# Opening stage of a hybrid decoder layer: load order, the engine that scales x, and instructions kept in program order

## The chip, the cores and the metric

The kernel runs on one core of one Trainium2 chip. The metric is the device time of one execution in microseconds; runs are compared by their medians. The core has five engines with an instruction queue each: PE (TensorE, matmuls), DVE (VectorE), ACT (ScalarE), POOL (GpSimd) and SP (SyncE, which here only issues DMAs). POOL issues DMAs too.

## The reference, cut to what matters

One decoder layer on x of shape 256 tokens x 2048 channels, all in float32. The part that the change touches computes the first normalised and modulated input u:

```python
mod = silu(c) @ w_mod + b_mod              # c: one row of 2048; w_mod: 2048 x 12288
shift1, scale1, ... = split(mod, 6)
u = rms(x, norm1_w) * (1.0 + scale1) + shift1
proj = u @ w_in                            # 2048 x 18464: q, k, v of both mixers, gates, b and a
qkv_b = silu(causal_depthwise_conv(proj[qkv], conv_w))
beta = sigmoid(proj[b]);  g = -exp(a_log) * softplus(proj[a] + dt_bias)
```

After it come two token mixers (stick-breaking attention and a gated delta rule), their merge through `p_a`, `p_b` and `w_out`, and a SwiGLU feed-forward part. Every element of the output depends on u.

## The kernel before, in words

All large products are done as three matmuls on pairs of reduced-precision parts. An operand `a` is split into `ah` (a cast, on ACT) and `al = a - ah` (a subtraction, on DVE). A weight block of 256 x 512 is loaded as `raw`, cast to `wh` (`split_hi`, line 304) and subtracted to `wl` (`split_lo`, through the helper at line 121). One such block is a **step**: 24 matmuls of 256 columns. `raw`, `wh` and `wl` have four buffers each, so the split of step n needs the matmuls of step n-4 to be finished. Buffers of one tag are handed out in program order: the cast of step n+1 is never issued ahead of the cast of step n.

`scale1` and `shift1` are wanted per channel, down the partitions, so they are not made by a wide matmul. Function `u_sums` loads w_mod block by block (`smod`, 512 KB each, issued by POOL at line 407, nine buffers) and adds it up on DVE with the entries of silu(c) as scalars: 16 sums for each of four quarters of the channels (`PIECES`). The even blocks go to `acc01`, the odd ones to `accb`. After the sixteenth sum of a quarter, 32 small matmuls with a column of ones (`pb_mod`) bring the sums to the partitions, and three small DVE operations finish `mcols`. `u_piece(p)` then applies them to the transposed x (`xT`) on ACT, casts to `uh` on ACT and subtracts to `ul` on DVE. I call the quarters 0 to 3, and the sums of quarter p "sum 0 to 15 of quarter p".

x itself is loaded (`xs`, 2 MB), squared and summed on ACT, the reciprocal root is taken on POOL (line 173), x is scaled (line 471, DVE), transposed by 32 matmuls (`pb_u`) and copied to `xT` by ACT (line 480). Small loads of the same stage are `wba` (the 32 columns of w_in for b and a: 2048 pieces of 128 bytes), `crow` (conv_w, transposed on PE to `cw`, copied by DVE at line 460) and `adt` (a_log, dt_bias).

The projections that need u while it is made are the **outer** steps of `run_jobs`, 36 in number. Steps 0 to 11 take channels 0 to 1023 for q, k and v of head group 1; at the ends of steps 9 to 11 their partial results are parked. Steps 12 to 35 take all channels for q, k and v of head group 0. `u_piece(0)` is written at step 0, `u_piece(1)` at step 6, `u_piece(2)` at step 24 and `u_piece(3)` at step 27 (`HK`); the first use of quarter 3 is at step 30. Between the matmuls of the outer steps the program writes the sums of the next quarter: three per step or a little fewer, one or two after each half step. For quarter 3, sums 0 to 2 are written in step 24, 3 to 5 in step 25, 6 and 7 in step 26, and 8 to 15 are written out in full by `u_piece(3)` in step 27. In each step n, the split of step n+1 is written first.

Step 33 finishes q of head group 0. Its `done` calls `open_phase` (masks, and `gdn_scalars`: small ACT, DVE and PE operations for beta and g, ending in the tables exp/ln) and then writes the whole convolution of that q: four ACT scalings, twelve DVE multiply-adds, two Silu on ACT (`gq`). The split of step 35 is written right after it, at the top of step 34.

The order in which each engine executes is set by a planner when the program is built: it issues an instruction on its engine as soon as its inputs are ready in the planner's own forecast of the run, and among several ready ones the first in the program. So an instruction may stand ahead of others that were written earlier. `tc.keep_in_program_order(ins)` puts `ins` behind the instruction that was written just before it on the same engine; nothing is said of the instructions around. An engine's queue, once planned, is executed strictly in that order. `xs` uses the same pool of six large buffers as `acc01` and `accb`, which are asked for earlier, so in the kernel before its load stands behind the first sums in the plan.

Of the kernel before, what the change touches and what calls it, by code (L numbers as in the profile page):

```python
# [38 lines left out]
H2 = 5  # L39
RG = 2  # L40
SMA = 8
NS0 = 4
NS1 = 4
PIECES = ((0, 4), (4, 4), (8, 4), (12, 4))
HK = (0, 0, 0, 2)
HOP = 3
# [51 lines left out]
def body(tc, cst, x, c, w_mod, b_mod, norm1_w, w_in, q_norm_w, k_norm_w, conv_w, a_log, dt_bias,  # L98
# [25 lines left out]
        nc.vector.scalar_tensor_tensor(out=o, in0=a, scalar=s, in1=b, op0=op0, op1=op1, **kw)  # L124

    def act(o, i, f, **kw):
        nc.scalar.activation(out=o, in_=i, func=f, **kw)

    def f32(t):
        return t.bitcast(F32)  # L130
# [158 lines left out]
    def run_jobs(jobs, bg_every=0, outer=(), bg_from=0):  # L289
        steps = [(j, q) for group in outer for q in range(group[0].kt // 2) for j in group]  # L290
        n_outer = len(steps)
        steps += [(j, q) for j in jobs for q in range(j.kt // 2)]
        ns = len(steps)
        raws, splits = {}, {}

        def load(n, queue=nc.sync):
            j, q = steps[n]
            r = wp.tile([P, 2, 512], F32, tag="raw", name="raw", bufs=RAWS)
            queue.dma_start(out=r, in_=j.w[j.kb * P + q * 256:j.kb * P + (q + 1) * 256, j.c0:j.c0 + 512].rearrange("(k p) n -> p k n", p=P))
            raws[n] = r  # L300

        def split_hi(n):
            wh = wp.tile([P, 2, 512], F32R, tag="wh", name="wh", bufs=WB)
            nc.scalar.copy(out=wh, in_=raws[n])  # L304
            splits[n] = (wh,)

        def split_lo(n):
            wl = wp.tile([P, 2, 512], F32R, tag="wl", name="wl", bufs=WB)
            wh = splits[n][0]
            tt(wl, raws.pop(n), f32(wh), ALU.subtract)  # L310
            if n + RAWS < ns:
                load(n + RAWS)
            splits[n] = (wh, wl)

        for n in range(min(RAWS, ns)):
            load(n, nc.gpsimd if outer and n >= RG else nc.sync)
        split_hi(0)
        split_lo(0)
        tick = 0
        for n, (j, q) in enumerate(steps):  # L320
            if n == n_outer:
                for i in range(1, SA):
                    split_hi(n + i)
                    split_lo(n + i)
            if q == 0:
                if j.before:
                    j.before()
                while len(convs) > 1:
                    pump_conv()
                j.acc = [bank("acc", j.tag) for _ in range(4 if j.wide else 2)]  # L330
            wh, wl = splits.pop(n)
            acc = j.acc
            own = n >= n_outer

            def beat(t):

                if own:
                    if t == SPA and n + SA < ns:
                        split_hi(n + SA)
                    if t == SPB and n + SA < ns:  # L340
                        split_lo(n + SA)
                    pump_conv()
                    pump(j.pump)

            if not own and n + 1 < ns and n + 1 not in splits:
                split_hi(n + 1)
                split_lo(n + 1)
            for kk in range(2):
                k = q * 2 + kk
                if k in j.hooks:  # L350
                    j.hooks[k]()
                ah, al = j.act()
                ka = j.kb + k
                first, last = k == 0, k == j.kt - 1
                for b in range(2):
                    beat(2 * kk + b)
                    if j.wide:

                        for cb in (2 * b, 2 * b + 1):
                            s = slice(cb * P, (cb + 1) * P)  # L360
                            mm(acc[cb], wh[:, kk, s], ah(ka), first, False)
                            mm(acc[cb][:, 0:T], wl[:, kk, s], al(ka), False, last)
                    elif j.chan:
                        for cb in (2 * b, 2 * b + 1):
                            o = acc[b][:, (cb % 2) * T:(cb % 2 + 1) * T]
                            s = slice(cb * P, (cb + 1) * P)
                            mm(o, wh[:, kk, s], ah[:, ka], first and cb % 2 == 0, False)
                            mm(o, wh[:, kk, s], al[:, ka], False, False)
                            mm(o, wl[:, kk, s], ah[:, ka], False, last)
                    else:  # L370
                        s = slice(b * P, (b + 1) * P)
                        mm(acc[b], ah[:, ka, s], wh[:, kk], first, False)
                        mm(acc[b], al[:, ka, s], wh[:, kk], False, False)
                        mm(acc[b], ah[:, ka, s], wl[:, kk], False, last)
                if n < n_outer and sums:
                    next(sums[0], None)
                    if tick % 3 == 0:
                        next(sums[0], None)
                if not own:
                    pump(j.pump)  # L380
                tick += 1
                if bg_every and j.bg and tick >= bg_from and tick % (bg_every if j.kt != KT or not j.wide else 2) == 0:
                    pump_bg()
            if q == j.kt // 2 - 1:
                j.done(acc)
# [27 lines left out]
    def u_sums(pi):  # L413
# [3 lines left out]
        for g in range(KT // kg):  # L417
            load_smod(SMA)
            t = smod[pi, g]
            smod[pi, g] = None  # L420
            for kk in range(kg):
                k = kg * g + kk
                a = (acc01, accb)[k % 2][:, :, c0:c0 + cn]
                if k < 2:
                    nc.vector.tensor_scalar(out=a, in0=t[:, :, kk], scalar1=cc[:, k:k + 1], scalar2=None, op0=ALU.mult)
                else:
                    stt(a, t[:, :, kk], cc[:, k:k + 1], a, ALU.mult, ALU.add)
            yield
        for i0 in range(0, kn, 2):
            pm = bank("pb_mod")  # L430
# [9 lines left out]
            tt(mcols[:, 1, kr], pm[:, 0:128:64], bsh1[:, kr], ALU.add)  # L440
        yield

    sums = [u_sums(0)]
    for _ in range(NS0):
        next(sums[0])
    xs = big.tile([P, NB, D], F32, tag="s16", name="xs")
    nc.sync.dma_start(out=xs, in_=xv)
    wba = tps.tile([P, KT, 32], F32, name="wba")
    nc.sync.dma_start(out=wba, in_=w_in[:, OFF_BA:OFF_BA + 32].rearrange("(k p) n -> p k n", p=P))
    for i in range(2):  # L450
        nc.sync.dma_start(out=crow[:, i], in_=conv_w.rearrange("a (k p) -> (a k) p", p=P)[i * 96:(i + 1) * 96])
    adt = cp.tile([P, 2, H], F32, name="adt")
    nc.sync.dma_start(out=adt[:, 0], in_=a_log.partition_broadcast(P))
    nc.sync.dma_start(out=adt[:, 1], in_=dt_bias.partition_broadcast(P))

    cw = cp.tile([P, 2, 96], F32, name="cw")
    pc = bank("pb_cw")
    for i in range(2):
        nc.tensor.transpose(pc[:, i * 96:(i + 1) * 96], crow[:, i], ident[:96, :96])
    nc.vector.tensor_copy(out=cw, in_=pc[:, 0:192])  # L460
    cwv = cw.rearrange("p a b -> p (a b)")

    ss = cp.tile([P, 4, 8], F32, name="ss")
    xT = s16("xT")
    rstd1 = cp.tile([P, 2], F32, name="rstd1")
    for b in range(NB):
        act(xT[:, b * 8:(b + 1) * 8].rearrange("p k t -> p (k t)"), xs[:, b], AF.Square, accum_out=ss[:, 0, b:b + 1])
    nc.vector.tensor_scalar(out=ss[:, 1, 0:2], in0=ss[:, 0, 0:2], scalar1=1.0 / D, scalar2=EPS, op0=ALU.mult, op1=ALU.add)
    rsqrt(rstd1, ss[:, 1, 0:2])
    for b in range(NB):  # L470
        nc.vector.tensor_scalar(out=xs[:, b], in0=xs[:, b], scalar1=rstd1[:, b:b + 1], scalar2=None, op0=ALU.mult)
    for _ in range(NS1):
        next(sums[0])
    for j in range(KT // 2):
        pt = bank("pb_u")
        for i in range(2):
            for b in range(NB):
                k = 2 * j + i
                tr(pt[:, i * T + b * P:i * T + (b + 1) * P], xs[:, b, k * P:(k + 1) * P])
        nc.scalar.copy(out=xT[:, 2 * j:2 * j + 2], in_=pt.rearrange("p (a t) -> p a t", t=T))  # L480

    wbah = tps.tile([P, KT, 32], F32R, name="wbah")
    wbal = tps.tile([P, KT, 32], F32R, name="wbal")
    nc.scalar.copy(out=wbah, in_=wba)
    tt(wbal, wba, f32(wbah), ALU.subtract)

    uh, ul = s16("uh", F32R), s16("ul", F32R)
    uact = lambda: (uh, ul)
# [3 lines left out]
    def u_piece(pi):  # L492
# [5 lines left out]
        for k in range(k0, k0 + kn, 2):  # L498
# [3 lines left out]
            k2 = slice(k, k + 2)  # L502
            nc.scalar.copy(out=uh[:, k2], in_=xT[:, k2])
            tt(ul[:, k2], xT[:, k2], f32(uh[:, k2]), ALU.subtract)
        if not pba:
            pba.append(bank("pb_ba"))
        o = pba[0][0:32, 0:T]
        for k in range(k0, k0 + kn):
            mm(o, wbah[:, k], uh[:, k], k == 0, False)
# [11 lines left out]
    def gdn_scalars():  # L521
# [16 lines left out]
        act(gs[:, 2], gs[:, 2], AF.Exp, scale=-1.0)  # L538
        act(gs[:, 2], gs[:, 2], AF.Ln, bias=1.0)
        stt(gs[:, 3], y, 0.0, gs[:, 2], ALU.max, ALU.add)  # L540
        act(ea, adt[:, 0], AF.Exp)
        stt(gt, gs[:, 3], -1.0, ea.unsqueeze(1).to_broadcast([P, NB, H]), ALU.mult, ALU.mult)
        nc.scalar.copy(out=gth, in_=gt)
        tt(gtl, gt, f32(gth), ALU.subtract)
# [865 lines left out]
```

## Time and profile before

| what | value |
|---|---|
| median of 3 runs | 2052.79 us (2048.81 to 2055.16) |
| the profiled execution's own time | 2056.12 us |
| its span | 2054.1 us |
| PE busy, share of the span | 1983.1 us, 97% |
| DVE, ACT busy | 1386.4 us, 1064.9 us |
| mean granted clock of PE | 0.991 |

The span is divided into stages with different limits. A busy share over the whole span says little of the first 200 us, in which DVE, PE and the DMA engines each are full for a time. Idle time of an engine counts only where what it delivers is waited for. Times in the rows are microseconds from the start of the span.

### The profile page before, as it was taken

What the parts mean: (1) busy time and instruction counts of PE and PEld (TensorE: products, weight loads), DVE (VectorE), ACT (ScalarE), POOL (GpSimd) and SP (SyncE); (2) the same over time, 40 slices, a digit from 0 to 9 for tenths busy, and PEclk for the clock granted to TensorE, in tenths of its full rate; (3) what the DMA queues carried; (4) which work ended last, traced back from release to release, by engine and by line L of the source; (5) the groups of instructions that cost most, each with busy time, mean ns of one, the idle gap of its engine ahead of it and who ended that gap; (6) DMA issues with size and microseconds to landing.
All of it is one profiled execution on the core that took longest, in us unless ns stands there. A gap on an engine that the chain in (4) does not pass through costs nothing.

```text
span 2054.1 us, 29271 instructions
## 1 busy us (share of the span) xinstructions
PE 1983.1 (97%) x11097; PEld 1720.7 (84%) x11097; DVE 1386.4 (67%) x1846; ACT 1064.9 (52%) x1766; POOL 108.9 (5%) x141
## 2 busy tenths in 40 slices
PE   1999999999999999999999999999999999999998
PEld 1899999897888888888888888788888888888887
DVE  4986979877676667447776877676775555556554
ACT  3346676776666667443454445554455334445432
POOL 4311011010000000000000000000000000000000
PEclk9899999999999999999999999999999999999999
DMA  8995533444776675768797888587875566665564
GB/s 302 386 336 184 160 126 116 125 122 142 240 229 197 223 232 165 222 193 284 253 309 257 301 320 277 178 269 239 268 244 185 195 193 188 188 189 186 186 214 134
DMA packets 208555, 449.72 MB, mean 219 GB/s; under 512 B 16103, under 2 KB 16538, under 8 KB 207902
## 3 DMA queue, kind: packets, MB, share of 16 engines
q1 hardware_dynamic: 198910, 413.25, 62.6%
q0 software_dynamic: 9504, 34.61, 4.5%
q8 instruction: 87, 1.43, 0.3%
q14 instruction: 54, 0.44, 0.1%
HBM read 445.70 MB, written 2.10 MB: 218 GB/s over the span
## 4 chain that ended last, share of the span: by engine, by line
PE 93%; DMA 3%; DVE 2%; issue 1%; ACT 1%; POOL 0%; SPq 0%; DVEq 0%; ACTq 0%; POOLq 0%
PE acc L118 85%; DMA smod<-in_w_mod 1%; DMA crow<-in_conv_w 1%; PE pb_mod L118 1%; PE pb_Q L118 1%; DMA raw<-in_w_in 0%; PE pb_oa L118 0%; PE pb_z L118 0%; PE pb_X L118 0%; DVE wl L121 0%; PE pb_af L118 0%; DVE accb L124 0%; PE pb_o L118 0%; PE pb_u L118 0%; PE pb_tr L140 0%
## 5 line engine op out<-in xcount | busy, mean ns | idle before, releaser
L121 DVE TENSOR_TENSOR wl<-raw,wh 128x1024 fp32r<-128x1024 f32 x648 | 791.8, 1224 | 515.4 <-ACT wh L304 513.8
L304 ACT CAST wh<-raw 128x1024 fp32r<-128x1024 f32 x648 | 680.2, 1050 | 776.7 <-PE acc L118 694.9
L118 PE MATMUL acc<-u,wh 128*128 128x512 f32 x1408 | 494.8, 396 | 0.0
L118 PE MATMUL acc<-u,wl 128*128 128x256 f32 x1408 | 395.3, 281 | 0.0
L118 PEld LDWEIGHTS acc<-u,wh 128*128 128x128 f32 x1408 | 264.2, 188 | 63.1
L118 PE MATMUL acc<-wh,uh 128*128 128x512 f32 x768 | 307.1, 400 | 0.0
L118 PE MATMUL acc<-wl,uh 128*128 128x512 f32 x768 | 300.6, 391 | 0.0
L118 PE MATMUL acc<-wh,ul 128*128 128x512 f32 x768 | 300.1, 391 | 0.0
L118 PEld LDWEIGHTS acc<-u,wl 128*128 128x128 f32 x1408 | 266.1, 189 | 0.2
L118 PE MATMUL acc<-uh,wh 128*128 128x256 f32 x768 | 221.3, 291 | 1.5 <-ACT part L955 1.5
L118 PE MATMUL acc<-ul,wh 128*128 128x256 f32 x768 | 218.8, 286 | 0.0
L118 PE MATMUL acc<-uh,wl 128*128 128x256 f32 x768 | 218.7, 286 | 0.0
L118 PE MATMUL acc<-wh,ff 128*128 128x512 f32 x704 | 216.9, 389 | 0.0
L118 PEld LDWEIGHTS acc<-wl,uh 128*128 128x128 f32 x768 | 144.5, 188 | 30.8
L118 PEld LDWEIGHTS acc<-wh,ul 128*128 128x128 f32 x768 | 144.8, 189 | 27.2
L118 PEld LDWEIGHTS acc<-wh,uh 128*128 128x128 f32 x768 | 144.7, 188 | 26.8
L118 PEld LDWEIGHTS acc<-wh,ff 128*128 128x128 f32 x704 | 132.0, 188 | 27.5
L118 PEld LDWEIGHTS acc<-uh,wh 128*128 128x128 f32 x768 | 148.6, 195 | 2.6 <-ACT part L955 1.7
L118 PEld LDWEIGHTS acc<-ul,wh 128*128 128x128 f32 x768 | 148.6, 193 | 0.6
L118 PEld LDWEIGHTS acc<-uh,wl 128*128 128x128 f32 x768 | 148.0, 193 | 0.4
L118 PE MATMUL acc<-wl,ff 128*128 128x512 f32 x352 | 137.0, 389 | 0.0
L202 DVE SCALAR_TENSOR_TENSOR macc<-wm,cols,macc 128x1024 f32<-128x1024 f32 x92 | 117.7, 1280 | 0.8 <-DMA wm<-in_w_mod 0.6
(289 smaller groups left out, 2269.2 us busy)
## 6 DMA issues: line engine op xcount, KB each, us to landing
raw<-in_w_in SPq DMA_DIRECT2D x286, 512.0 KB, 4.2
wm<-in_w_mod SPq DMA_DIRECT2D x128, 512.0 KB, 5.6
raw<-in_w_gate SPq DMA_DIRECT2D x88, 512.0 KB, 4.5
raw<-in_w_up SPq DMA_DIRECT2D x88, 512.0 KB, 4.4
raw<-in_w_down SPq DMA_DIRECT2D x88, 512.0 KB, 4.3
smod<-in_w_mod POOLq DMA_DIRECT2D x64, 512.0 KB, 11.4
raw<-in_p_a SPq DMA_DIRECT2D x32, 512.0 KB, 4.9
raw<-in_p_b SPq DMA_DIRECT2D x32, 512.0 KB, 5.0
```

Source lines behind the costliest of these rows:

```text
L118: nc.tensor.matmul(o, lhsT=lhsT, rhs=rhs, start=start, stop=stop, skip_group_check=True)
L121: nc.vector.tensor_tensor(out=o, in0=a, in1=b, op=op)
L202: ins = nc.vector.scalar_tensor_tensor(out=acc, in0=t, scalar=cc[:, k:k + 1], in1=acc, op0=ALU.mult, op1=ALU.add)
L304: nc.scalar.copy(out=wh, in_=raws[n])
```

## The change

The load of x is issued first, in two halves, one per 128 tokens, and ahead of the sums in the program. The small loads `wba`, `crow` and `adt` are moved into `u_piece(0)`, so that in the program they come after the first four weight blocks; their casts, the transposes of `crow` and the copy of `cw` are moved into `u_piece(1)`, and the matmuls of b and a for quarter 0 are done there together with those of quarter 1. x is scaled by ACT in place of DVE. The number of sums written ahead of the normalisation goes from 4 to 5, and of those written after it from 4 to 8; these 8 now come behind the transposes. And many instructions are put in program order: the squares, the scaling, the copies to `xT`, all sums, and the two splits of every outer step (`n < n_outer`), the small splits and one exp.

```diff
         def split_hi(n):
-            nc.scalar.copy(out=wh, in_=raws[n])
+            ins = nc.scalar.copy(out=wh, in_=raws[n])
+            if n < n_outer:
+                tc.keep_in_program_order(ins)
...
         def split_lo(n):
-            tt(wl, raws.pop(n), f32(wh), ALU.subtract)
+            ins = nc.vector.tensor_tensor(out=wl, in0=raws.pop(n), in1=f32(wh), op=ALU.subtract)
+            if n < n_outer:
+                tc.keep_in_program_order(ins)
...
                 if k < 2:
-                    nc.vector.tensor_scalar(out=a, in0=t[:, :, kk], scalar1=cc[:, k:k + 1], ...)
+                    ins = nc.vector.tensor_scalar(out=a, in0=t[:, :, kk], scalar1=cc[:, k:k + 1], ...)
                 else:
-                    stt(a, t[:, :, kk], cc[:, k:k + 1], a, ALU.mult, ALU.add)
+                    ins = nc.vector.scalar_tensor_tensor(out=a, in0=t[:, :, kk], ...)
+                tc.keep_in_program_order(ins)
...
+    pin = tc.keep_in_program_order
+    xs = big.tile([P, NB, D], F32, tag="s16", name="xs")
+    for b in range(NB):
+        nc.sync.dma_start(out=xs[:, b], in_=xv[:, b])
     sums = [u_sums(0)]
     for _ in range(NS0):
         next(sums[0])
-    nc.sync.dma_start(out=xs, in_=xv)
...
     for b in range(NB):
-        nc.vector.tensor_scalar(out=xs[:, b], in0=xs[:, b], scalar1=rstd1[:, b:b + 1], ...)
-    for _ in range(NS1):
-        next(sums[0])
+        pin(act(xs[:, b], xs[:, b], AF.Copy, scale=rstd1[:, b:b + 1]))
     for j in range(KT // 2):
...
-        nc.scalar.copy(out=xT[:, 2 * j:2 * j + 2], in_=pt.rearrange("p (a t) -> p a t", t=T))
+        pin(nc.scalar.copy(out=xT[:, 2 * j:2 * j + 2], in_=pt.rearrange("p (a t) -> p a t", t=T)))
+    for _ in range(NS1):
+        next(sums[0])
...
+    def small_loads():          # wba, crow twice, adt twice
+    def small_splits():         # wbah (ACT), wbal (DVE), crow's transposes, cw (DVE), pinned
...
-        if not pba:
+        if pi == 0:
+            small_loads()
+            return
+        if pi == 1:
+            small_splits()
             pba.append(bank("pb_ba"))
+            k0, kn = 0, k0 + kn
...
-        act(ea, adt[:, 0], AF.Exp)
+        pin(act(ea, adt[:, 0], AF.Exp))
```

## Rows read from the trace of the kernel before

**Rows 1.** The page: busy tenths of PE and of the DMA engines in 40 slices.
```profile
PE   1999999999999999999999999999999999999998
DMA  8995533444776675768797888587875566665564
```

**Rows 2.** By stretch: length; busy PE, PEld, DVE, ACT, POOL; clock, DMA share, GB/s.
```profile
0.00:28.00 28.00, 1.05 (x3) 0.55 (x3) 5.69 (x10) 5.29 (x7) 10.02 (x20) 1.00 0.95 316
36.00:38.00 2.00, 0.00 (x0) 0.00 (x0) 2.00 (x2) 0.77 (x1) 1.92 (x2) 1.00 0.00 0
28.00:56.00 28.00, 10.61 (x64) 9.93 (x64) 22.42 (x28) 14.27 (x20) 13.41 (x17) 1.00 0.84 303
56.00:80.00 24.00, 22.20 (x171) 21.45 (x171) 23.44 (x21) 6.81 (x9) 10.68 (x15) 0.93 1.03 386
80.00:90.00 10.00, 8.89 (x43) 8.18 (x42) 7.14 (x14) 4.21 (x7) 2.33 (x5) 0.51 1.03 387
51.19:108.52 57.33, 51.49 (x379) 49.58 (x379) 52.73 (x61) 21.81 (x30) 23.11 (x32) 0.88 1.03 386
```

**Rows 3.** SP's issues in the first 25 us: start, duration, what.
```profile
4.41 0.40 SPq L449 DMA_DIRECT2D wba<-in_w_in  x1
4.86 12.87 SPq L451 DMA_DIRECT2D crow<-in_conv_w  x2
20.37 0.70 SPq L447 DMA_DIRECT2D xs<-in_x  x1
```

**Rows 4.** The way of x in time: ACT, POOL, DVE, PE; idle before in brackets.
```profile
31.00 1.91 ACT L127 ACTIVATE xT<-xs 128x2048 f32<-128x2048 f32 x1 [4.55 <-DMA xs<-in_x]
34.80 1.98 ACT L304 CAST wh<-raw 128x1024 fp32r<-128x1024 f32 x2
36.08 1.60 POOL L173 TENSOR_TENSOR rstd<-ss,half 128x2 f32<-128x2 f32 x1 [6.98 <-DVE ss L468]
41.72 2.51 DVE L471 TENSOR_SCALAR xs<-xs,rstd 128x2048 f32<-128x2048 f32 x2
43.10 6.95 PE L140 MATMUL pb_u<-cs,xs 128*128 128x128 f32 x32 [16.61 <-DVE xs L471]
```

**Rows 5.** DVE in time: the copy of cw, sums, splits, ul at the quarters' ends.
```profile
26.53 0.36 DVE L460 COPY cw<-pb_cw 128x192 f32<-128x192 f32 x1 [12.85 <-PE pb_cw L459]
49.91 1.28 DVE L124 SCALAR_TENSOR_TENSOR accb<-smod,cols,accb 128x1024 f32<-128x1024 f32 x1 [3.41 <-DMA smod<-in_w_mod]
56.69 1.38 DVE L121 TENSOR_TENSOR ul<-xT,uh 128x512 fp32r<-128x512 f32 x2
59.18 1.28 DVE L124 SCALAR_TENSOR_TENSOR accb<-smod,cols,accb 128x1024 f32<-128x1024 f32 x1
60.38 1.28 DVE L124 SCALAR_TENSOR_TENSOR acc<-smod,cols,acc 128x1024 f32<-128x1024 f32 x1
107.24 1.29 DVE L124 SCALAR_TENSOR_TENSOR accb<-smod,cols,accb 128x1024 f32<-128x1024 f32 x1
152.67 1.28 DVE L124 SCALAR_TENSOR_TENSOR accb<-smod,cols,accb 128x1024 f32<-128x1024 f32 x1
```

**Rows 6.** ACT's casts of outer steps in time, with what ended the wait; the splits' count.
```profile
150.32 1.05 ACT L304 CAST wh<-raw 128x1024 fp32r<-128x1024 f32 x1 [3.20 <-PE acc L118]
166.77 1.05 ACT L304 CAST wh<-raw 128x1024 fp32r<-128x1024 f32 x1 [2.44 <-PE acc L118]
175.41 1.05 ACT L304 CAST wh<-raw 128x1024 fp32r<-128x1024 f32 x1 [1.83 <-PE acc L118]
L121 DVE TENSOR_TENSOR wl<-raw,wh x35: 1217/1224/1233, 35.9 to 173.6; 128x1024 fp32r<-128x1024 f32 x35
```

**Rows 7.** The convolution of step 33's q in time: first scaling, last multiply-add, last Silu.
```profile
180.57 1.57 ACT L127 ACTIVATE gq<-acc,cw 128x256 f32<-128x256 f32 x4 [1.23 <-PE acc L118]
189.46 0.47 DVE L124 SCALAR_TENSOR_TENSOR gq<-acc,cw,gq 128x253 f32<-128x253 f32 x1
190.77 0.63 ACT L127 ACTIVATE gq<-gq 128x512 f32<-128x512 f32 x1
```

More of the change, by code (lines that the diff above doesn't have):

```diff
@@ L41 @@
 SMA = 8
-NS0 = 4
-NS1 = 4
+NS0 = 5
+NS1 = 8
 PIECES = ((0, 4), (4, 4), (8, 4), (12, 4))
@@ L126, in act @@
     def act(o, i, f, **kw):
-        nc.scalar.activation(out=o, in_=i, func=f, **kw)
+        return nc.scalar.activation(out=o, in_=i, func=f, **kw)
     def f32(t):
@@ L424, in u_sums @@
                 if k < 2:
-                    nc.vector.tensor_scalar(out=a, in0=t[:, :, kk], scalar1=cc[:, k:k + 1], scalar2=None, op0=ALU.mult)
+                    ins = nc.vector.tensor_scalar(out=a, in0=t[:, :, kk], scalar1=cc[:, k:k + 1], scalar2=None, op0=ALU.mult)
                 else:
-                    stt(a, t[:, :, kk], cc[:, k:k + 1], a, ALU.mult, ALU.add)
+                    ins = nc.vector.scalar_tensor_tensor(out=a, in0=t[:, :, kk], scalar=cc[:, k:k + 1], in1=a, op0=ALU.mult, op1=ALU.add)
+                tc.keep_in_program_order(ins)
             yield
@@ L445, in body @@
         next(sums[0])
-    xs = big.tile([P, NB, D], F32, tag="s16", name="xs")
-    nc.sync.dma_start(out=xs, in_=xv)
[L448 to L461, printed above, removed]
     ss = cp.tile([P, 4, 8], F32, name="ss")
@@ L466, in body @@
     for b in range(NB):
-        act(xT[:, b * 8:(b + 1) * 8].rearrange("p k t -> p (k t)"), xs[:, b], AF.Square, accum_out=ss[:, 0, b:b + 1])
-    nc.vector.tensor_scalar(out=ss[:, 1, 0:2], in0=ss[:, 0, 0:2], scalar1=1.0 / D, scalar2=EPS, op0=ALU.mult, op1=ALU.add)
+        pin(act(xT[:, b * 8:(b + 1) * 8].rearrange("p k t -> p (k t)"), xs[:, b], AF.Square, accum_out=ss[:, 0, b:b + 1]))
+    pin(nc.vector.tensor_scalar(out=ss[:, 1, 0:2], in0=ss[:, 0, 0:2], scalar1=1.0 / D, scalar2=EPS, op0=ALU.mult, op1=ALU.add))
     rsqrt(rstd1, ss[:, 1, 0:2])
     for b in range(NB):
-        nc.vector.tensor_scalar(out=xs[:, b], in0=xs[:, b], scalar1=rstd1[:, b:b + 1], scalar2=None, op0=ALU.mult)
-    for _ in range(NS1):
-        next(sums[0])
+        pin(act(xs[:, b], xs[:, b], AF.Copy, scale=rstd1[:, b:b + 1]))
     for j in range(KT // 2):
@@ L479, in body @@
                 tr(pt[:, i * T + b * P:i * T + (b + 1) * P], xs[:, b, k * P:(k + 1) * P])
-        nc.scalar.copy(out=xT[:, 2 * j:2 * j + 2], in_=pt.rearrange("p (a t) -> p a t", t=T))
+        pin(nc.scalar.copy(out=xT[:, 2 * j:2 * j + 2], in_=pt.rearrange("p (a t) -> p a t", t=T)))
+    for _ in range(NS1):
+        next(sums[0])
+    wba = tps.tile([P, KT, 32], F32, name="wba")
+    adt = cp.tile([P, 2, H], F32, name="adt")
+    cw = cp.tile([P, 2, 96], F32, name="cw")
+    cwv = cw.rearrange("p a b -> p (a b)")
+    def small_loads():
+        nc.sync.dma_start(out=wba, in_=w_in[:, OFF_BA:OFF_BA + 32].rearrange("(k p) n -> p k n", p=P))
+        for i in range(2):
+            nc.sync.dma_start(out=crow[:, i], in_=conv_w.rearrange("a (k p) -> (a k) p", p=P)[i * 96:(i + 1) * 96])
+        nc.sync.dma_start(out=adt[:, 0], in_=a_log.partition_broadcast(P))
+        nc.sync.dma_start(out=adt[:, 1], in_=dt_bias.partition_broadcast(P))
+    def small_splits():
+        pin(nc.scalar.copy(out=wbah, in_=wba))
+        pin(nc.vector.tensor_tensor(out=wbal, in0=wba, in1=f32(wbah), op=ALU.subtract))
+        pc = bank("pb_cw")
+        for i in range(2):
+            nc.tensor.transpose(pc[:, i * 96:(i + 1) * 96], crow[:, i], ident[:96, :96])
+        pin(nc.vector.tensor_copy(out=cw, in_=pc[:, 0:192]))
     wbah = tps.tile([P, KT, 32], F32R, name="wbah")
     wbal = tps.tile([P, KT, 32], F32R, name="wbal")
-    nc.scalar.copy(out=wbah, in_=wba)
-    tt(wbal, wba, f32(wbah), ALU.subtract)
     uh, ul = s16("uh", F32R), s16("ul", F32R)
```

## The prediction

> **What bounds the kernel now.** I read the slices first [rows 1]: PE is full in 38 of 40 and nearly idle in the first, so nothing behind the opening can give much, and whatever shifts PE there shifts the end by as much. Next the stretches [rows 2]. The reader is to see three things. The DMA engines are not idle before 56 us (316 and 303 GB/s), but they stand still for a moment (0 GB/s at 36 to 38) while POOL waits for the reciprocal root [rows 4]; from 56 us they run at 386. DVE is busy for 52.73 of the 57.33 us between the last sum of quarter 0 and that of quarter 2, so in that stretch it is DVE that paces PE. And PE's clock falls once to 0.51. Then the queues in order of time: SP puts wba and the two crow loads ahead of x, and x is issued only at 20.37 [rows 3]. DVE stands still for 12.85 us before the copy of cw, which waits for crow [rows 5]. The last sum of quarter 0 ends at 49.91 + 1.28 = 51.19 [rows 5]. Last, ACT's casts of the outer steps [rows 6]: from 166.77 to 175.41 three steps pass, 2.88 us each, and every cast waits for PE, so from there PE sets the pace and the casts run ahead of it.
>
> **The change, part by part.** Four terms.
>
> *Opening.* The 12.85 us wait of DVE goes with the copy of cw, and POOL's wait of 6.98 us shrinks, since x comes first [rows 4, 5]. What is late next? Two things, and I work out both. The chain of x: issue at 4.41 in wba's place [rows 3]; from issue to the first square it took 31.00 - 20.37 = 10.6 us behind crow, and 2.1 MB at 386 GB/s [rows 2] would take 5.4, so it lands between 10 and 15; the second square ends two microseconds later at the most. The next DVE operation on the way now stands behind five sums; five blocks of 0.52 MB and x are 4.7 MB, at 316 GB/s [rows 2] 15 us, so about 19 to 20. Reciprocal root 1.60 [rows 4]: 21.7. Scaling on ACT: no row shows it; the nearest is the square of the same shape at 1.91, so 3.8 in place of 2.51 on DVE [rows 4] (between 2.5 and 5): 25.5. Transposes 6.95 and one copy of about 0.6: 33. Now the casts of steps 0 and 1 stand behind the copies (1.98 [rows 4]), their subtractions behind sum 12 and ahead of sums 13 to 15: 36. Three sums, 1.20 apart [rows 5], end near 40. The other way is bytes: sixteen blocks (8.4 MB), x (2.1), four weight blocks (2.1) and half a megabyte of small loads are 13.1 MB, 34 us at 386 or 41 at 316 GB/s [rows 2], and 2 us of start: 36 to 43, plus one sum. I take 42 for the end of quarter 0 in place of 51.19: 9.2 us won (6 to 13).
>
> The Trainium skill ("DMA: Bandwidth & Descriptors", Specifications) gives about 358 GB/s as one core's limit at HBM. By it the 13.1 MB would take 37 us and the gain would be some 11 us at most; the trace shows 386 over 24 us, so the measurement decides.
>
> *Quarters 1 and 2 on DVE.* Before, the last sum of quarter 2 ended at 108.53 [rows 5], 57.3 us after that of quarter 0; 52.7 of it were work, 4.6 idle [rows 2]. Now the first sum of a quarter stands behind the `ul` of the quarter before. The two `ul` end at 58.07 [rows 5], 6.9 us after the last sum, and of these DVE's own work (`ul` 1.38, small operations 0.7) fills 2.1. Before, first sums and splits filled most of the rest; now 4.8 stay idle, at two boundaries 9.6. That is 5.0 more than the 4.6 of before. The small splits come on top: the copy of cw (0.36) and a subtraction of half a split's size, 1.0 together. The splits themselves keep their number and only change places. Sum: 57.3 + 5.0 + 1.0 = 63.3, so quarter 2 ends at 105.3: 3.2 us won of the 9.2 (0 to 6). Here PE takes over as the bound, so I carry 3.2 on as PE's shift.
>
> *Quarter 3.* Before, its sums floated ahead into DVE's free time and the last ended at 153.95 [rows 5]. Now sums 3 to 15 are tied to the splits of steps 26 to 28, and the split of 26 needs the end of step 22, for want of a buffer. Counted from the end of step 22: cast and split 2.3; sums 3 to 5, 3.6; a split, 1.2; two sums, 2.4; a split, 1.2; eight sums, 9.6: 20.3. Then from the last sum to the second cast of u: in quarter 0 the `ul` that follows it ended 6.9 after the sum, so 6.2; then the cast of step 29, now behind it, 1.05. So step 29 starts 27.6 after the end of step 22. Before, the cast at 150.32 marks the end of step 24 and that at 166.77 the end of step 28 [rows 6] (each waits for a buffer from four steps earlier): 16.45 for four steps, with the small matmuls in them. Steps 23 and 24 are 2 x 2.88 and twelve small matmuls, 7.1: 23.6 in all. The stall is 4.0 us (2 to 8: nothing hides the chain on the low side but matmuls that PE can take early; at half clock the small matmuls double). The loss comes on DVE's order, not its load.
>
> *Step 35.* 35 splits are done by 173.6, so the cast at 175.41 is that of step 35 [rows 6], 8.6 us before PE needs it: it marks the end of step 31, and three more steps end at 184.0. After the change it is written behind the convolution of step 33's q and is pinned there, behind the last Silu on ACT and the last multiply-add on DVE. Casts keep their order, so those of steps 36 and on wait too, and PE has nothing to do ahead. The convolution starts at 180.57 and its last Silu ends at 191.40 [rows 7]. In between DVE also did two splits (2.4), which now come later: 189.0 at best. With a cast of 1.05 the weights stand ready between 190.1 and 192.5, against 184.0: a stall of 6.1 to 8.5. If the planner puts the q convolution ahead of the small gate operations, 5. I take 6.5 (4 to 9).
>
> Edits that cost nothing: the pinned exp (16 columns, beside PE's steps), the later b and a matmuls (the same twelve and twelve), x in two DMAs (SP has nothing else to issue then). Crow's and wba's bytes stay in the first 40 us; SP stands in their issue, as for 12.87 now [rows 3], but the next weight load waits for the first split in any case.
>
> **Sum.** -3.2 + 4.0 + 6.5 = +7.3 us. The profiled execution took 2056.12 (span 2054.1), 3.3 above the median of the runs shown; with the change it would be 2063.4. From the median 2052.79 the sum gives 2060. About 0.3%, 6.2 us, is what can be told from no change here, so the forecast is just over that line.
>
> **The rivals.**
>
> *A, the other side: the tail stalls don't come.* If quarter 3's sums still run ahead and the split of step 35 isn't late, the opening decides alone. For it: PE's slices are full there [rows 1], so the plan of before found room for all of it. Against it: the text of the change pins sums and splits alike. The gain is then between 3.2 and 9.2: 2047 (2043 to 2050). It decides as soon as DVE's order costs less than 3 us behind 108 us.
>
> *B, one of the two stalls.* Quarter 3's chain hides under early matmuls, or PE finds other work at step 35. Then -3.2 + 4.0 or + 6.5: 2053 to 2056, no change.
>
> *C, the clock too.* PE's clock was 0.51 at 80 to 90 [rows 2], after PE had waited for quarter 1's last sum; that is the lower of the two levels, 1.2 of 2.4 GHz, and 8.89 us of busy time there did the work of 4.5. After two new waits of 4 and 6.5 us the same would follow, once or twice 2 to 4 us: 2066. A plan that still puts the small loads ahead of x, so that the change doesn't do what it says, loses the 3.2 and ends near 2064, in the same place.
>
> The Trainium skill ("TensorE: Matmul & The Clock Gate", Part 1) says that the clock is halved when PE has been idle and is given back under sustained work. By that rule both waits would be followed by half speed and the sum would be some 6 us more, which is rival C; the trace agrees in the one place where PE had waited.
>
> **How the numbers follow.** Forecast 0.38, A 0.20, B 0.25, C 0.17. The forecast's own range is 2056 to 2065. Faster by over 0.3% (below 2046.6) is A's better half and a little of its rest: 0.15. Within: the rest of A, all of B and a third of the forecast: 0.37. Slower (above 2059): 0.48. The range leaves out A's better half below and the far part of C above: 2046 to 2067.
>
> **What would show it.** Right: x issued near 4.4 with the small loads behind it; the last sum of quarter 0 ending near 42 and of quarter 2 near 105; PE waiting 2 to 8 us ahead of step 29 for a cast that stands behind quarter 3's `uh`; and PE waiting 5 to 8 us ahead of step 35, with ACT's cast right behind the second Silu of gq. Wrong: PE full from 110 us on, or quarter 0 ending after 47, or a wait of DVE for the copy of cw as before.

## The result: 0.8% slower, twice the forecast's loss

| | median | ratio to before | 
|---|---|---|
| before (beside the changed kernel) | 2053.2 us (4 runs, 2048.81 to 2055.16) | |
| changed | 2069.15 us (4 runs, 2069.01 to 2069.99) | 1.0079 [1.0064, 1.0094] |

The forecast was 2060 (2046 to 2067): slower is right, the size is not, and the time lies outside the range. The profiled execution took 2069.21, span 2067.4, 13.3 more than the span before.

### The profile page after: what moved, and what is told of

It is laid out like the page before. It is cut to its first block, busy times and chain, and to the rows that moved or that the text cites. A ratio compares the mean times of both kernels' runs of the same rounds, so it can differ in the third digit from the quotient of the medians.

```text
span 2067.4 us, 29277 instructions
## 1 busy us (share of the span) xinstructions
PE 1995.2 (97%) x11097; PEld 1732.6 (84%) x11097; DVE 1384.3 (67%) x1844; ACT 1071.0 (52%) x1768; POOL 107.2 (5%) x141
## 4 chain that ended last, share of the span: by engine, by line
PE 93%; DVE 2%; DMA 2%; issue 1%; ACT 1%; SPq 0%; POOL 0%; DVEq 0%; ACTq 0%; POOLq 0%
PE acc L118 85%; DMA smod<-in_w_mod 1%; PE pb_mod L118 1%; PE pb_Q L118 1%; DMA xs<-in_x 1%; PE pb_u L140 1%; PE pb_oa L118 0%; PE pb_z L118 0%; PE pb_X L118 0%; PE pb_af L118 0%; PE pb_o L118 0%; PE pb_u L118 0%; PE pb_tr L140 0%; PE pb_kk L118 0%; PE pb_qk L118 0%
## 5 line engine op out<-in xcount | busy, mean ns | idle before, releaser
L118 PE MATMUL acc<-uh,wh 128*128 128x256 f32 x768 | 225.4, 296 | 10.5 <-ACT wh L304 7.6
```

Of the source, the lines that this page charges most:

```text
L118: nc.tensor.matmul(o, lhsT=lhsT, rhs=rhs, start=start, stop=stop, skip_group_check=True)
```

## The profile after

The page's slices: PE, its granted clock and the DMA engines in 40 slices of the span.

```profile
PE   3898999999999999999999999999999999999998
PEclk8898999999999999999999999999999999999999
DMA  9994533434667666667887888487775566656564
```

A slice is 51.7 us. Against [rows 1] PE has work in the first slice already, but the second and the fourth (155 to 207 us), full before, are at 8, with the clock at 8 too. In the second PE is still ahead of the kernel before; the loss is to be looked for in the fourth. The opening in time (start, duration, engine, line, what; idle before and its releaser in brackets), picked from SP, ACT and DVE:

```profile
4.43 0.93 SPq L453 DMA_DIRECT2D xs<-in_x  x2
8.43 25.69 SPq L485 DMA_DIRECT2D crow<-in_conv_w  x2
22.32 3.90 ACT L127 ACTIVATE xs<-xs,rstd 128x2048 f32<-128x2048 f32 x2 [2.02 <-POOL rstd L173]
37.99 1.28 DVE L431 SCALAR_TENSOR_TENSOR accb<-smod,cols,accb 128x1024 f32<-128x1024 f32 x1
42.62 0.23 DVE L121 TENSOR_TENSOR mcols<-pb_mod,cols 128x2 f32<-128x2 f32 x2 [3.34 <-PE pb_mod L118]
45.60 0.23 DVE L121 TENSOR_TENSOR mcols<-pb_mod,cols 128x2 f32<-128x2 f32 x2 [2.63 <-PE pb_mod L118]
71.52 1.29 DVE L431 SCALAR_TENSOR_TENSOR accb<-smod,cols,accb 128x1024 f32<-128x1024 f32 x1
105.86 1.28 DVE L431 SCALAR_TENSOR_TENSOR accb<-smod,cols,accb 128x1024 f32<-128x1024 f32 x1
```

x is issued first, the wait for `cw` [rows 5] is gone, and quarter 0's last sum ends at 39.27 in place of 51.19. But quarter 2's ends at 107.14 in place of 108.53 [rows 5]: of 11.9 us won, 1.4 are left. Next the stretches (length; busy PE, PEld, DVE, ACT, POOL; granted clock, DMA share, GB/s):

```profile
28.00:56.00 28.00, 19.73 (x113) 19.15 (x112) 19.62 (x24) 11.92 (x18) 10.68 (x15) 0.70 1.05 369
56.00:80.00 24.00, 18.32 (x121) 17.46 (x120) 18.65 (x22) 4.74 (x6) 8.09 (x12) 0.82 1.03 386
159.80:171.20 11.40, 8.81 (x46) 7.12 (x45) 4.42 (x11) 5.24 (x9) 2.44 (x6) 0.67 0.15 46
171.20:175.30 4.10, 4.10 (x27) 4.10 (x26) 4.10 (x5) 2.58 (x6) 0.00 (x0) 0.67 0.63 176
190.00:195.50 5.50, 0.63 (x7) 0.53 (x5) 5.29 (x15) 5.04 (x12) 0.00 (x0) 0.90 0.00 0
195.50:201.00 5.50, 5.46 (x25) 5.44 (x26) 5.41 (x6) 3.52 (x5) 0.00 (x0) 0.50 0.58 172
```

In [rows 2] one stretch of 10 us stands near half clock. Here the mean is 0.70 and 0.82 in the first two stretches, and lower again in 160 to 175 and from 195.5. The reader is to see the last two rows: PE stands almost still for 5.5 us, and then works 5.46 us at 0.50, the lower of its two levels (1.2 of 2.4 GHz). That is step 35. Its cause is in ACT's queue, in time, and PE's first matmul of the step:

```profile
186.29 1.57 ACT L127 ACTIVATE gq<-acc,cw 128x256 f32<-128x256 f32 x4 [6.99 <-PE acc L118]
193.92 0.63 ACT L127 ACTIVATE gq<-gq 128x512 f32<-128x512 f32 x1 [0.30 <-DVE gq L124]
194.45 3.87 ACT L304 CAST wh<-raw 128x1024 fp32r<-128x1024 f32 x4
195.54 0.58 PE L118 MATMUL acc<-uh,wh 128*128 128x256 f32 x1 [4.91 <-ACT wh L304]
```

ACT was idle for 6.99 us ahead of the convolution's first scaling; before, the cast of step 35 ran in that time [rows 6]. Now it stands right behind the second Silu, with three more casts behind it. The other place is the end of quarter 3 (DVE, ACT and PE rows; two small matmuls to a PE row):

```profile
148.39 1.05 ACT L304 CAST wh<-raw 128x1024 fp32r<-128x1024 f32 x1 [3.20 <-PE acc L118]
160.10 1.28 DVE L431 SCALAR_TENSOR_TENSOR accb<-smod,cols,accb 128x1024 f32<-128x1024 f32 x1
162.60 0.39 PE L118 MATMUL pb_mod<-cs,acc 128*128 128x64 f32 x2
163.25 0.23 DVE L121 TENSOR_TENSOR mcols<-pb_mod,cols 128x2 f32<-128x2 f32 x2 [1.87 <-PE pb_mod L118]
165.30 0.63 PE L118 MATMUL pb_mod<-cs,acc 128*128 128x64 f32 x2
167.25 0.23 DVE L121 TENSOR_TENSOR mcols<-pb_mod,cols 128x2 f32<-128x2 f32 x2 [3.64 <-PE pb_mod L118]
169.29 3.89 ACT L304 CAST wh<-raw 128x1024 fp32r<-128x1024 f32 x4
```

From 149.4 to 169.3 ACT makes no cast of weights, because the next one is pinned behind quarter 3's `uh`. The small matmuls change speed inside the chain: a row of two takes 0.39 us (the next starts 0.22 later), then 0.63 (0.43 later).

Counting 24 matmuls to a step in both traces (a matmul or two of them can be off, 0.2 us) gives how far PE is behind the kernel before:

| first matmul of | before | after | behind | forecast |
|---|---|---|---|---|
| step 0 | 56.45 | 47.22 | -9.2 | -9.2 |
| step 23 | 143.11 | 141.18 | -1.9 | -3.2 |
| step 29 | 166.69 | 171.24 | +4.55 | +0.8 |
| step 30 | 169.57 | 175.29 | +5.7 | +0.8 |
| step 34 | 181.41 | 187.14 | +5.7 | +0.8 |
| step 35 | 184.40 | 195.54 | +11.1 | +7.3 |
| step 36 | 187.72 | 200.92 | +13.2 | +7.3 |
| step 61 | 285.47 | 300.27 | +14.8 | +7.3 |

## Experiments

The kernel before ran beside each: median 2054.78 (29 runs) with the first four, 2054.06 with the next four, 2054.04 with e9 to e12, 2053.53 with the last two. The changed kernel was not run again beside them, so a difference against its 2069.15 also holds the spread of the kernel before between the batches (2053.2 to 2054.8): it is good to some 2 us.

**e1, e2, e3: the two pinned places, one by one and together.**

```diff
-            if n < n_outer:
+            if n < n_outer - 1:        # e1 and e3, in split_hi and split_lo
...
-                tc.keep_in_program_order(ins)
+                if pi < 3:             # e2 and e3, in u_sums
+                    tc.keep_in_program_order(ins)
```

> The split of step 35 alone is no longer kept in program order; all else as in the changed kernel. Theory P (the pin puts the cast behind the convolution): step 35 starts 2.9 to 3.3 us after step 34 instead of 8.4, and PE's half clock behind it goes too (step 35 to 36 took 5.4 instead of 3.3): 5.4 + 2.1 = 7.5 us less, 2061.7. Rival W (the convolution's own work is the limit, the stall only moves to steps 36 to 39): 2067 to 2069. Rival T (the time is given back by later waits, so a stall here never reached the end): above 2067, with step 36 as early as under P.

> The sums of quarter 3 alone are no longer kept in program order. Theory P: the last sum of quarter 3 ends before 150 instead of 161.4, step 29 follows step 28 without the 11.4 us of small matmuls and waits in a row, and the half clock in steps 29 and 30 goes: 6.45 + 1.2 = 7.7 us less, 2061.5; the wait ahead of step 35 stays (5.4). Rival S (the splits 26 to 28 stay behind the sums written before them, so the floating sums still hold them up): half of it, 2065. Rival T (given back later): above 2067.

> Both: quarter 3's sums and the split of step 35 free. Theory P, two independent terms: 7.5 + 7.7 = 15.2 us less than the changed kernel, 2054.0, which is the time of the kernel before within what can be told; PE full from 120 to 240. Rival W: one of the two terms comes back in another place, 2060 to 2062.

| | median | ratio to before | against the changed kernel |
|---|---|---|---|
| e1 | 2058.93 | 1.0016 [1.0007, 1.0026] | -10.2 |
| e2 | 2060.54 | 1.0027 [1.0017, 1.0037] | -8.6 |
| e3 | 2052.29 | 0.9988 [0.9979, 0.9998] | -16.9 |

Theory P holds, with more behind it than was expected of each. PE's lag at step 61, read as in the table above, says the same: 9.2, 9.1 and 16.5 us less than in the changed kernel. In e1 the cast of step 35 is back in ACT's idle time ahead of the convolution, and the cast of step 36 follows it at 183.83:

```profile
180.95 1.05 ACT L304 CAST wh<-raw 128x1024 fp32r<-128x1024 f32 x1 [1.83 <-PE acc L118]
186.11 1.57 ACT L127 ACTIVATE gq<-acc,cw 128x256 f32<-128x256 f32 x4 [1.23 <-PE acc L118]
```

Both places together hold the whole loss: without them the new opening is 2.5 us ahead of before.

**e4, e8: fewer pins.** e4 pins the sums of quarter 0 and the splits of steps 0 and 1 alone (`if pi == 0`, `if n < 2`), e8 no sum and no split.

> Only the sums of quarter 0 and the splits of steps 0 and 1 are kept in program order; the new loads and the scaling on ACT stay. Theory P: the opening keeps its 9 us at step 0 (47 instead of 56.5); at the two boundaries between quarters DVE has sums and splits again while it waits for the small matmuls (after: 2.21 + 2.63 idle at the second, 3.34 + 2.63 at the first), some 5 us more than in the run with both free: 2049, faster than before by 4. Rival D (the transfers set the pace: DMA engines are full from 28 to 110 us in both kernels, so order on DVE can give at most what the earlier start of the transfers gives, about 2): 2052 to 2054.

> The changed kernel without any pin on sums and splits; the new load order, the scaling on ACT and its pins stay. Theory P: the same as with only quarter 0 pinned, since the sums of quarter 0 come in the order of their transfers anyway: 2052. Rival Q (without pins the first splits run ahead of quarter 0's last sums, or x's way gets behind sums again): step 0 at 50 or later and 2054 to 2056.

e4: 2052.39, 0.9993 [0.9983, 1.0002]. e8: 2052.06, 0.9991 [0.9982, 1.0000]. For e4 theory P's 2049 did not come, rival D's 2052 to 2054 did. For e8 theory P's 2052 came, and not the losses of rival Q. In e8 step 0 starts at 42.96, 13.5 us ahead of before, and step 6 at 83.3, 1.2 ahead: the lead goes within quarter 1. Its rows on DVE and ACT, and then its chain of waits (start, length, what):

```profile
58.84 1.23 DVE L312 TENSOR_TENSOR wl<-raw,wh 128x1024 fp32r<-128x1024 f32 x1 [8.20 <-ACT wh L304]
61.64 1.06 ACT L304 CAST wh<-raw 128x1024 fp32r<-128x1024 f32 x1 [2.83 <-DMA raw<-in_w_in]
```

```profile
37.28 20.41 DMA raw<-in_w_in
57.76 1.05 ACT wh L304
75.48 6.25 PE pb_mod L118 x28
```

A weight block is on its way for 20.41 us; its cast comes at 57.76, and DVE stands 8.2 us for it with the next sums behind it. The next cast (61.64) waits for its transfer as well. This spoke for the transfers (rival D), so e12 tests that alone, on e8.

**e12: fewer bytes.** Quarter 1 loads only the half of each w_mod block for `shift1` and reads it twice; the half for `scale1` is left out.

```diff
-            if kg == 1:
+            if pi == 1:
+                nc.gpsimd.dma_start(out=t[:, 0, 0], in_=src[:, 0, 0, c0:c0 + cn])
+            elif kg == 1:
...
+                tk = t[:, 0:1, kk].to_broadcast([P, 2, cn]) if pi == 1 else t[:, :, kk]
```

> The kernel without pins on sums and splits, but quarter 1 loads only the half of each w_mod block for shift1 and reads it twice (the scale half is left out; the work of every engine is the same): 4.2 MB less, 10.9 us at 386 GB/s. Theory D (the transfers eat what the opening wins: weight blocks land 18 to 20 us after their issue there and DVE stands 8.2 us for one): that wait goes, quarter 1's last sum moves from 75.4 to 68 to 70, step 6 from 83.3 to 77 to 79, and 3 to 5 us of it stay: 2047 to 2049. Rival K or order (half clock and DVE's order set the pace): step 6 not before 82, 2051 to 2052.

2041.95, 0.9942 [0.9928, 0.9955]: 10.1 less than e8, more than theory D asked for. Step 6 starts at 73.3, 10.0 earlier. The 4.2 MB left out are 10.9 us at 386 GB/s, so nearly all of their time comes through to the end: with x ahead and no pins, transfers set the pace of the opening. With the pins of the changed kernel this was not run. Its chain of waits has no transfer between quarter 0's end and quarter 1's; these are its longest pieces there:

```profile
37.48 1.79 PE pb_mod L118 x14
43.06 12.80 PE acc L118 x92
65.44 6.25 PE pb_mod L118 x28
```

**e5, e13, e14: the clock behind the two waits.** Extra matmuls in the changed kernel, e5 behind step 34, e13 behind the last two sums of quarter 3, e14 both.

```diff
+            if n == n_outer - 2:
+                junk = bank("pb_fill")
+                for _ in range(40):
+                    tc.keep_in_program_order(nc.tensor.matmul(junk[:, 0:T], lhsT=onesr, rhs=uact()[0][:, 0], ...))
...
+                if pi == 3 and k >= 14:
+                    mm(bank("pb_fill"), ident, a[:, 0])
```

> The changed kernel with 40 extra matmuls (256 columns, the kind of the steps, results unused) kept behind the last one of step 34, so that PE works through the wait ahead of step 35; at 0.12 us each they take 4.8 of its 5.4 us. Theory K (the half clock in step 35 follows from PE's wait): the granted clock of the stretch behind the wait is 1.0 instead of 0.50, step 35 to 36 takes 3.3 us instead of 5.4, and 2067 comes out instead of 2069.2. Rival M (step 35 is slow because its splits come late one by one): the fill does nothing but push, 2069 to 2071, with 5.4 us between steps 35 and 36 as before.

> The changed kernel with one extra matmul (128x512, float32, 0.89 us, result unused) behind each of the last two sums of quarter 3, in PE's short gaps between the end of step 28 and the small matmuls. Theory K: the clock is kept, all pairs of small matmuls take 0.22 us (the second half took 0.43), those of b and a 0.12 instead of 0.21, and step 29 has full speed: 1.8 + 1.0 + 1.2 less and 0.9 more for the fill itself, 3 us less than 2069.15: 2066. Rival N (the stretch of small matmuls loses the clock itself, with or without a fill ahead of it): pairs at 0.43 again and 2069 to 2070.

> Both fills, quarter 3 and the wait ahead of step 35, in the changed kernel. Theory K, two independent shares (3.3 measured for step 35, 3 expected for quarter 3): 2063. That would be the two waits without their half clock, 3 above the forecast's 2060. Rival N: as the run that fills the wait ahead of step 35 alone, 2066.

e5: 2065.86, 1.0058 [1.0046, 1.0070], 3.3 less than the changed kernel, with a wait of the same length. The fill and the stretch behind it:

```profile
189.20 4.91 PE L391 MATMUL pb_fill<-uh,rmask 128*128 128x256 f32 x40
```

```profile
196.00:202.00 6.00, 5.70 (x48) 5.50 (x47) 6.00 (x11) 4.40 (x9) 0.00 (x0) 1.00 0.89 290
```

Clock 1.00 where it was 0.50, and 3.4 us from step 35 to 36 in place of 5.4, 2.0 less: theory K. The other 1.3 of the 3.3 come behind step 36 (see the account of the sum, below). e13: 2068.64, 1.0072 [1.0058, 1.0086], and e14: 2065.61, 1.0058 [1.0045, 1.0070], as rival N had it, no better than e5. In e13 the small matmuls keep full clock to their end, but the fall only comes later, in those of b and a:

```profile
165.66 0.39 PE L118 MATMUL pb_mod<-cs,acc 128*128 128x64 f32 x2
168.65 0.41 PE L118 MATMUL pb_ba<-uh,wbah 128*32 128x256 f32 x1
```

Step 30 starts at 175.5 as before the fill (175.3): what the pairs gain the fill itself costs. For quarter 3 both theories missed (K in the time, N in the pairs); that step 29's half clock can be had back was not shown.

**e6, e9: the clock at the quarters' ends.** Both on e4, with extra matmuls behind the transposes of x (six, then nine); e9 also behind the last seven sums of quarter 1.

```diff
+    for _ in range(6):                 # e9: 9
+        pin(nc.tensor.matmul(junk, lhsT=ident, rhs=xs[:, 0, 0:512], ...))
...
+                if pi == 1 and k >= 9:         # e9 alone
+                    mm(bank("pb_fill"), ident, a[:, 0])
```

> The kernel with only quarter 0 pinned, and six extra matmuls (128x512, float32, results unused) kept behind the transposes of x, to bridge PE's 6.5 us idle time ahead of quarter 0's small matmuls. Theory K: the small matmuls run at full clock (a pair in 0.22 us instead of 0.43), step 0 starts 2.7 to 3.4 us after the first of them less late, near 45.5 instead of 49.0, and steps 0 and 1 lose their half clock. What it is worth at the end: if the order on DVE and the clock set the opening's pace, 2 to 3 us less than 2052.4: 2049.5; rival D (the transfers do, the DMA engines are full from 28 to 110 us): step 6 starts at 81 to 82 as before and the time stays 2052.

> As the run that filled quarter 0, with nine extra matmuls instead of six (0.89 us each, so that they reach the small matmuls; six ended 2.63 us short of them), and in quarter 1 one extra matmul of the same size behind each of its last seven sums. Results unused. Theory K: with PE at work up to the small matmuls, a pair of them takes 0.22 us instead of 0.43 at both boundaries; the way from the last sum to step 0 and to step 6 gets 2.7 us shorter each (7.95 and 7.9 before), 2 to 4 us less than 2052.4 at the end. Rival D (transfers): step 6 earlier by less than 1, same time. Rival N (the small matmuls do not hold the clock themselves, as ahead of step 29, where PE came straight from full work and still fell to half): pairs at 0.43 again, same time.

e6: 2052.06, 0.9990 [0.9982, 0.9998], no change to e4. The fill ended 2.63 us too early. The first small matmuls behind that gap still run at full clock (four in 0.63), but from 39.65 on a row of two takes 0.64 again:

```profile
38.05 0.63 PE L118 MATMUL pb_mod<-cs,acc 128*128 128x64 f32 x4 [2.63 <-DVE acc L431]
40.08 0.64 PE L118 MATMUL pb_mod<-cs,acc 128*128 128x64 f32 x2
```

e9: 2050.56, 0.9985 [0.9976, 0.9994]: without that gap all take 0.39, at both boundaries:

```profile
40.05 0.39 PE L118 MATMUL pb_mod<-cs,accb 128*128 128x64 f32 x2
47.26 1.65 PE L118 MATMUL acc<-uh,wh 128*128 128x256 f32 x6 [4.59 <-ACT uh L522]
76.55 0.39 PE L118 MATMUL pb_mod<-cs,acc 128*128 128x64 f32 x2
```

Yet step 0 is no earlier than with six (47.26): `mcols` is ready sooner, but in ACT's queue a weight cast that waits for its transfer stands ahead of u:

```profile
43.72 1.04 ACT L304 CAST wh<-raw 128x1024 fp32r<-128x1024 f32 x1 [11.00 <-DMA raw<-in_w_in]
```

Step 6 comes at 79.8 (e4: 81.5) and step 14 at 110.3 (113.1). But e10, below, has 80.3 and 111.8 without any fill, and its time is only 1.1 us longer: what the fills are worth at the end is not clear of the noise. e9 is the fastest full version run, 3.5 us ahead of before.

**e7: the pins without the new opening.** The kernel before, with all sums and the outer splits pinned.

> The kernel before with the pins alone: its old load order and x scaled on DVE, but all sums and the two splits of every outer step kept in program order. Theory P: the two stalls come as in the changed kernel (7 to 9 us ahead of step 29 and 8 to 10 at step 35, the half clock behind them counted in) and nothing is won at the opening: 2054.8 + 17 = 2072. Rival O (the stalls come from the earlier opening, which lets PE run ahead of DVE, and not from the pins): 2055 to 2060.

2082.82, 1.0140 [1.0127, 1.0153]: worse than both theories. The stalls come without the new opening (step 28 to 29 takes 12.6 us, 34 to 35 8.4), so rival O falls. What neither had: pinned sums also stand behind x's way on DVE, and step 0 starts at 63.4, 7 us later than before:

```profile
35.24 0.17 DVE L473 TENSOR_SCALAR ss<-ss 128x2 f32<-128x2 f32 x1 [7.50 <-ACT xT L127]
40.85 1.28 DVE L431 SCALAR_TENSOR_TENSOR acc<-smod,cols,acc 128x1024 f32<-128x1024 f32 x1
```

With these pins, then, and across two batches, the rest of the change is worth 13.7 us (2082.8 to 2069.15); without them some 2 (e8).

**e10, e11: the other parts of the opening.** On e4: x scaled on DVE; the small loads ahead of x.

> Only quarter 0 pinned, and x scaled on DVE (2.51 us for both halves, behind the fifth sum) instead of ACT (3.9). If the place of the scaling matters, quarter 0's last sum comes 1 to 2.5 us later and the time is 2053 to 2055; if the transfers of quarter 0 set its pace (DVE waits for each of its sums there), no change: 2052.

> Only quarter 0 pinned, and the small loads issued ahead of x, as in the kernel before. Theory: x is issued near 20 instead of 4.4, so that pinned sums stand behind its way; step 0 at 60 to 63 instead of 49, and with quarter 1 then paced by DVE alone 5 to 8 us of it reach the end: 2058 to 2061. Rival D (transfers absorb it, as they absorbed the gain): 2052 to 2055.

e10: 2051.66, 0.9989 [0.9980, 0.9999], the same as e4: the engine that scales x does not matter. e11: 2057.25, 1.0012 [1.0003, 1.0021], 4.9 more than e4, between the two theories; step 0 is 7.7 later there and step 6 2.1.

## Why the forecast was right in sign and wrong in size

**The opening: right to step 0, then for another reason.** x's way was forecast well: second square done at 20.2 (19 to 20), root by 22.3 (21.7), scaled by 26.2 (25.5). Quarter 0's last sum came at 39.27 rather than 42, but the small matmuls behind it ran at half clock and took 2.7 of the 11.9 back, so that step 0 won the 9.2 of the forecast by luck. The next term, -3.2 for quarters 1 and 2, measured -1.9 in the trace and -2.5 by e3. DVE's idle time at the two boundaries was there, 7.7 and 6.5 us (3.34 + 2.63 + two waits for `uh`, and 2.21 + 2.63 + two), not 4.8 each, since the small matmuls took 0.43 a pair. But undoing the order there (e4, e8) gave nothing that can be told from e3: where DVE does not set the pace, the transfers do (e12, without pins). [rows 2] had shown them full, 1.03 and 386 GB/s from 56 us on; the forecast took DVE alone for the pace there.

**Quarter 3: the mechanism exact, the price not.** The forecast had the last sum 20.3 us after the end of step 22; it came at 161.38 - 141.18 = 20.2. From there it priced 7.3 to step 29, as in quarter 0 of the kernel before. It took 9.9: eight rows of small matmuls were 0.21 slower each, 1.7, and those of b and a ran at 0.21 instead of 0.12. Then step 29 itself lost 1.2 at half clock.

**Step 35: the mechanism exact.** The cast stands right behind the second Silu, as written. The wait was 5.4, forecast 6.5. Behind it step 35 lost 2.1 at half clock.

**The step that failed is the sum.** "-3.2 + 4.0 + 6.5" takes both waits as bare waits; the runs price them, with all that follows, at 8.6 and 10.2, together 16.9 in place of 10.5. The two traces split it: 2.5 more inside quarter 3's chain, where the small matmuls went at half clock, 1.2 and 2.1 in the steps behind the waits, 1.6 more between steps 36 and 61, and 1.1 less at step 35 than forecast: 10.5 + 2.5 + 3.3 + 1.6 - 1.1 = 16.8, and PE falls back by 16.7 from step 23 to step 61. The 1.6 are half clock as well, a third place, where PE has waited for `gw` of the gated delta rule that runs beside the steps:

```profile
252.15 0.49 PE L118 MATMUL pb_X<-gw 128*64 128x64 f32 x8 [2.17 <-ACT gw L717]
252.60:255.80 3.20, 3.20 (x16) 3.20 (x16) 1.97 (x5) 1.19 (x4) 0.00 (x0) 0.50 0.08 12
```

Neither e1 nor e2 has these 1.6, though e2 has the same wait (2.19 us at 242 to 245, clock 1.00); why the clock falls behind the one and not behind the other stays open. Since e1 and e2 each win them back, 10.2 and 8.6 add up to more than 16.9. So the missing term is the half clock, some 7 us in three places. It had its rival, C, with 2066 and a chance of 0.17; it was no case of its own but a part of the forecast, for both waits leave PE idle. e5 had 3.3 of it back: 2.0 in step 35, and the third place too, where it waits 1.3 us for `gw` and keeps 1.00. The Trainium skill ("TensorE: Matmul & The Clock Gate", Part 1) says that idle time halves the clock; by its rule the sum was 6 more, and e5 agrees with it for the wait ahead of step 35. Of the half clock in quarter 3's chain and in step 29, 3.7 us, only the trace speaks: e13 moved it and did not remove it.

**Readings of the trace before.** The forecast let PE's clock fall once [rows 2]. It was low at least twice in this time; the 0.93 of 56 to 80 us hides a stretch at half clock, again behind a wait of PE:

```profile
56.24 0.42 PE L118 MATMUL pb_ba<-uh,wbah 128*32 128x256 f32 x1 [1.65 <-ACT uh L503]
57.00:58.00 1.00, 1.00 (x7) 0.91 (x7) 1.00 (x3) 0.34 (x1) 0.00 (x0) 0.50 1.03 385
```

So 80 to 90 us was not the one place where PE had waited, and the clock had a place in the sum. Nor does POOL wait for the root at 36 to 38: it works it out there (36.08, 1.60 us), and its wait is the 6.98 us ahead of it [rows 4].

**Rivals A and B** fell: both stalls came. A's time, 2047, was too good as well: without the stalls the opening is worth 2.5 (e3) and not 3.2 to 9.2.

## What to carry to other kernels

A pin puts an instruction behind the one written just before it on its engine, and so behind all that this one stands and waits for: before pinning, list what the program writes ahead of it, and let the last steps of a range, where other work begins, float (here one split cost some 10 us). A wait on PE can cost its length and then slow work behind it (here 5.4 us and 2.1 more); put the second into the sum. Where the transfers are full, an opening that loads one thing earlier gains no more than the bytes behind it allow: look at the DMA share right behind the place, and ask what is left to win there before shortening any engine's way.

## What the runs showed that was not expected

- Small matmuls of 64 columns ran at 0.22 us a pair when PE came to them from full work (162.60, and e9), and at 0.43 from the fourth row on when it had stood 2.63 us ahead of them (e6). In quarter 3 they fell from one to the other on the way, with PE busy 8.81 of 11.40 us.
- SP stood 25.69 us in the two crow issues, with x and w_mod on the way, against 12.87 before [rows 3].
- With w_mod blocks in flight ahead of it, a 512 KB weight block took 20.41 us from its issue on (e8).
- The transfers of one core held 386 GB/s over 57 us [rows 2]. The Trainium skill ("DMA: Bandwidth & Descriptors", Specifications) gives about 358 as one core's limit at HBM; under Bandwidth the Trainium skill says there that this is about what each core gets with both cores of an HBM domain streaming. This kernel runs on one.
